# Three edits to a hybrid layer kernel: other step sizes in the down projections, wider column sums, two weight splits earlier

## The chip, the cores and the metric

One core of one Trainium2 chip runs the whole kernel in one launch. The metric is the time of an execution on the device in microseconds (us); less is better.

## What is computed

A decoder layer for 1024 tokens of width 1024, batch 1, all in float32. Each of its two feed-forward halves, with 2816 hidden columns, is

```python
def swiglu(h, w_gate, w_up, w_down):
    return (jax.nn.silu(h @ w_gate) * (h @ w_up)) @ w_down

def rms_norm(x, gain):
    xf = x.astype(jnp.float32)
    y = xf * lax.rsqrt(jnp.mean(xf * xf, axis=-1, keepdims=True) + EPS)
    return (y * gain.astype(jnp.float32)).astype(x.dtype)
```

The first half (stage 0) is followed by a mixer (four gated DeltaNet heads and four causal pooling groups), then by the second half (stage 1) and a final RMS norm. Every part is modulated by a vector c (adaLN).

## The kernel before

**Products in float32.** An operand is split into a high half of type fp32r, written by a cast on ScalarE (ACT) or GpSimd (POOL), and the low rest, which VectorE (DVE) writes as a subtraction. TensorE (PE) then issues three matmuls for each product of tiles: high × high, high × low, and low weights × high. They are one instruction each of 128x512 columns; a weight tile has a "split" with both halves.

**Seven products.** Gate, up and down are done as a 2 × 2 block scheme with seven products instead of eight (SLOTS: p1, p2, p5, p6, p3, p7, q4, in the order in which PE does them). The blocks of weights are combined on DVE (tiles pm, from raw or cv, which hold loaded blocks). The products go to PSUM banks: p1, p6, p7 and q4 use one bank of `mm` in turn, p2 a bank of `po`, p5 another, and p3 accumulates in p5's bank. So p6 waits until p1's content was read, p7 for p6's read, q4 for p7's, and p3 for p5's (the `flag("read", ...)` lines in `seven`).

**Pairs.** The 2816 hidden columns are 22 tiles, 11 pairs of tiles. Gate and up make one pair after the other, pair 1 first (PAIR0) and then in the order of PAIRS; the seven combinations of each pair's activation, split in halves, are what down multiplies. For the two pairs that are made last (DIRECT) DVE and ACT write these splits straight into their places in SBUF (`direct_task`): p5's into tiles U (high) and zs (low), p6 and p7 into G tiles, the others into H tiles. The other pairs' splits go to DRAM (`part_task`) and come back by DMA (`feed_task`). The eleventh pair is treated apart.

**Down.** It goes in steps. Step t works on the output pair d = t mod 4 with up to four pairs of hidden tiles; `nk` is the number of pairs. In the plan of before the steps have 1, 2, 3, 4, then 4, 4, 4, 4, then 4, 4, 3, 2 and 1 pairs. PE's row of products runs on from step to step, with the q4 of a step behind the p1 of the next. `down_read` lets DVE read a bank, scale it and add it to a residual tile A, which must have been loaded (`rest_load`, from `xpark` in stage 0 and from `rest` in stage 1); the tile that it is loaded into comes from a pool that activations use before.

**Order.** A planner in the program (`Order`), with costs for each operation and a rank for each task, decides before anything runs in which order each engine gets its instructions; each engine then takes them in that order. SyncE (SP) issues nearly all DMAs, also in a fixed order.

**Column sums.** For a norm the squares are summed over the width, which lies over partitions: `column_sums` multiplies a tile of 128x128 by ones on PE. In the finish (`finish`) there are three such sums of partial tiles for each group of rows, in separate columns, added by a reduction on DVE, followed by DVE's scale, POOL's power and the output. In `norm_task` there is one.

**Splits of weights.** `splits_task` spawns the tasks that split the weights ahead of PE (`unit_split`); a smaller rank is served sooner. The list `units` is that of the pair made first; its last two are the two halves of the up weights for the second tile of pair 1.

Of the kernel before, what the change touches and what calls it, by code (L numbers as in the profile page):

```python
# [11 lines left out]
ALU = mybir.AluOpType  # L12
AX = mybir.AxisListType

P = 128
D = 1024
# [10 lines left out]
PAIR0 = 1  # L27
PAIRS = (3, 4, 5, 6, 7, 8, 9, 10, 0, 2)

# [113 lines left out]
def hybrid_layer_kernel(  # L143
# [165 lines left out]

    def column_sums(parts, ps):  # L310
        for n in range(parts[0].shape[1] // P):
            for e, t in enumerate(parts):
                PE.matmul(ps[:, n : n + 1], lhsT=t[:, n * P : (n + 1) * P], rhs=ones[:, 0:1], start=(e == 0), stop=(e == len(parts) - 1))

# [437 lines left out]
    for st in range(2):  # L752
# [6 lines left out]
        for t in range(2 * NS):  # L759
            d = t % 4  # L760
            hi = min(NS, t + 1, at[d] + 4)
            if at[d] < hi:
                todo.append({"kind": "d", "d": d, "lo": at[d], "nk": hi - at[d], "w": wd})
                at[d] = hi
# [481 lines left out]
    def finish(st):  # L1246
# [3 lines left out]
        groups = ((0, 1), (1, 0))[i % 2]  # L1250
        kept = {}
        for g, b in enumerate(groups):
            banks = {}
# [9 lines left out]
            if g == 0:  # L1263
                yield flag("wrow")
                for m in range(n):
# [4 lines left out]
                    put(tags[m])  # L1270
        yield need("rec")
        sums = bank("rec")
        for j, e in enumerate((KT - 3, KT - 2, KT - 1)):
            yield flag("square", i, e)
            yield ("PE", 0.22 * n)
            column_sums((st["parts"][j - 1] if j else st["acc"],), sums[:, j * n : (j + 1) * n])
            put("cv" if j else "U")
        yield ("V", 0.3)
        r = small.tile([P, 4], F32, tag="rx", bufs=2, name=nm("rx"))[:, :n]
        V.tensor_reduce(r, sums[:, 0 : 3 * n].rearrange("p (j m) -> p m j", m=n), axis=AX.X, op=ALU.add)  # L1280
        V.tensor_scalar(r, r, 1.0 / D, EPS, op0=ALU.mult, op1=ALU.add)
        put("rec")
# [93 lines left out]
    def splits_task(units):  # L1376
        yield flag("w0", 1, 1, 1)
        yield from seven_splits(0)
        for key in [("last", dp) for dp in range(4)] + list(range(len(units))):
            yield need("split")  # L1380
            spawn(unit_split(key), 3)
        yield from seven_splits(1)
# [30 lines left out]
    def norm_task(h, i, parts, src, rank):  # L1413
# [5 lines left out]
        ps = bank("aux")  # L1419
        column_sums(parts[:1], ps)  # L1420
        yield ("V", 0.07)
        r = small.tile([P, 4], F32, tag="rx", bufs=2, name=nm("rx"))
        V.tensor_scalar(r, ps[:, 0:4], 1.0 / D, EPS, op0=ALU.mult, op1=ALU.add)
        put("aux")
# [658 lines left out]
```

## Time and profile before

| | |
|---|---|
| median of 3 runs | 1847.37 us (1847.31 to 1850.77) |
| the profiled execution | 1846.01 us |
| its span, first to last instruction | 1844.3 us |
| busy: PE, DVE, ACT, POOL | 97%, 76%, 41%, 15% of the span |
| mean granted clock of PE | 0.995 of full speed |

The profile is of one execution, so sums that are made from it stand against 1846.01. A name in it is that of the tiles without buffer numbers: `po<-H,split` is a matmul into a bank po with moving tile H and weight tile split. Nearly all operations are recorded by one helper and so have the same line (L161); stretches of time and names of tiles tell them apart. In timelines, equal neighbours are one row with a count.

### The profile page before, as it was taken

To read this page: it belongs to the slowest core of one execution; us is meant where nothing else is said; L and a number is where in the kernel's file an instruction comes from. 1 tells how busy PE (TensorE), PEld (TensorE's weight loads), DVE (VectorE), ACT (ScalarE), POOL (GpSimd) and SP (SyncE) were. 2 spreads that over 40 slices of the span, in tenths; PEclk is the share of its full clock that TensorE was granted. 3 is DMA by queue.
4 is the path that set the end of the run, shared out by engine and by line. 5 is a ranking of instruction groups with operands and counts; after the bars stand their busy time and mean duration, and the time that the engine had idled before them with its cause. 6 is when DMAs were issued, how large, how long until landed. Compare 5 with 4: busy or idle time off the path is not lost.

```text
span 1844.3 us, 25086 instructions
## 1 busy us (share of the span) xinstructions
PE 1793.7 (97%) x8527; PEld 1481.1 (80%) x8527; DVE 1398.6 (76%) x2434; ACT 759.9 (41%) x1504; POOL 283.5 (15%) x224
## 2 busy tenths in 40 slices
PE   7999999999899999999999999999999999999998
PEld 6788878888788877788888878878878888778877
DVE  5997888887778878988787666677787666786666
ACT  5454444454322224662443254354445444422223
POOL 2221121201100003120211122212111111100003
PEclk9999999999999999999999999999999999999999
DMA  9534665674679832331111155334455543667722
GB/s 323 176 126 162 221 220 191 189 236 127 201 248 329 302 102 98 103 79 43 31 48 49 41 172 157 99 120 145 153 186 180 181 141 116 207 206 254 237 77 98
DMA packets 307807, 293.81 MB, mean 159 GB/s; under 512 B 28061, under 2 KB 215506, under 8 KB 307680
## 3 DMA queue, kind: packets, MB, share of 16 engines
q1 hardware_dynamic: 307136, 291.09, 49.8%
q8 instruction: 67, 1.10, 0.2%
q0 software_dynamic: 544, 1.13, 0.2%
q14 instruction: 60, 0.49, 0.1%
HBM read 209.05 MB, written 83.10 MB: 158 GB/s over the span
## 4 chain that ended last, share of the span: by engine, by line
PE 84%; DVE 11%; issue 2%; ACT 1%; POOL 1%; DMA 1%; DVEq 0%; POOLq 0%; ACTq 0%
PE mm L161 47%; PE po L161 27%; PE aux L161 7%; PE rec L161 3%; DVE pm L161 2%; DVE split L161 2%; DVE A L161 2%; DVE ad L161 2%; DVE G L161 1%; DVE cv L161 1%; DVE H L161 1%; ACT A L161 0%; DMA G<-in_gdn_norm 0%; DVE zs L161 0%; ACT junk L161 0%
## 5 line engine op out<-in xcount | busy, mean ns | idle before, releaser
L161 PE MATMUL mm<-H,split 128*128 128x512 f32 (+1 forms) x3096 | 762.7, 394 | 10.5 <-DVE H L161 4.0
L161 PEld LDWEIGHTS mm<-H,split 128*128 128x128 f32 x3096 | 568.1, 189 | 127.7 <-issue 5.8
L161 PE MATMUL po<-H,split 128*128 128x512 f32 x1584 | 388.2, 392 | 4.5 <-DVE H L161 3.0
L161 PEld LDWEIGHTS po<-H,split 128*128 128x128 f32 x1584 | 297.1, 188 | 69.5 <-DVE H L161 4.2
L161 PE MATMUL mm<-G,split 128*128 128x512 f32 x1440 | 343.0, 390 | 4.3 <-ACT split L161 4.3
L161 PEld LDWEIGHTS mm<-G,split 128*128 128x128 f32 x1440 | 270.0, 188 | 61.2 <-ACT split L161 5.2
L161 ACT CAST split<-pm 128x512 fp32r<-128x512 f32 (+3 forms) x264 | 151.7, 582 | 329.0 <-DVE pm L161 321.7
L161 POOL TENSOR_TENSOR A<-A,A 128x512 f32<-128x512 f32 x80 | 131.9, 1659 | 690.8 <-DVE A L161 584.7
L161 DVE TENSOR_TENSOR split<-pm,split 128x512 fp32r<-128x512 f32 (+3 forms) x264 | 176.6, 676 | 45.1 <-ACT split L161 44.5
L161 ACT CAST split<-raw 128x512 fp32r<-128x512 f32 (+2 forms) x199 | 117.6, 595 | 193.0 <-PE mm L161 105.4
L161 PE MATMUL po<-U,split 128*128 128x512 f32 x480 | 155.5, 390 | 2.1 <-DVE A L161 2.0
L161 DVE SCALAR_TENSOR_TENSOR A<-mm,fg,A 128x512 f32<-128x512 f32 (+1 forms) x144 | 103.2, 719 | 63.6 <-PE mm L161 62.3
L161 DVE TENSOR_TENSOR split<-raw,split 128x512 fp32r<-128x512 f32 (+2 forms) x199 | 132.3, 675 | 21.4 <-ACT split L161 21.0
L161 DVE TENSOR_TENSOR A<-A,A 128x512 fp32r<-128x512 f32 (+1 forms) x180 | 124.1, 697 | 4.4 <-ACT A L161 1.2
L161 PEld LDWEIGHTS po<-U,split 128*128 128x128 f32 x480 | 90.1, 188 | 21.9 <-issue 1.7
L161 ACT CAST split<-cv 128x512 fp32r<-128x512 f32 (+1 forms) x96 | 57.1, 595 | 94.3 <-PE po L161 50.4
L161 DVE TENSOR_TENSOR A<-A,po 128x512 f32<-128x512 f32 x86 | 58.8, 684 | 46.4 <-PE po L161 43.7
L161 PE MATMUL po<-zs,split 128*128 128x512 f32 x240 | 93.4, 389 | 0.0
L161 DVE SCALAR_TENSOR_TENSOR ad<-ad,cs,ad 128x512 f32<-128x512 f32 x98 | 82.7, 844 | 3.2 <-DMA ad<-in_w_ada 2.4
L161 DVE TENSOR_TENSOR split<-cv,split 128x512 fp32r<-128x512 f32 (+1 forms) x96 | 62.7, 653 | 27.6 <-ACT split L161 27.6
L161 ACT CAST A<-A 128x512 fp32r<-128x512 f32 x120 | 72.8, 620 | 25.5 <-DVE A L161 25.2
L161 DVE SCALAR_TENSOR_TENSOR A<-po,fg,A 128x512 f32<-128x512 f32 x78 | 58.1, 749 | 32.2 <-PE po L161 31.5
(270 smaller groups left out, 1857.2 us busy)
## 6 DMA issues: line engine op xcount, KB each, us to landing
gd<-A SPq DMA_DIRECT2D x240, 256.0 KB, 3.9
H<-gd SPq DMA_DIRECT2D x144, 256.0 KB, 4.0
ad<-in_w_ada SPq DMA_DIRECT2D x112, 256.0 KB, 3.2
raw<-in_ffn_gate SPq DMA_DIRECT2D x88, 256.0 KB, 4.0
cv<-in_ffn_up SPq DMA_DIRECT2D x80, 256.0 KB, 4.3
G<-gd SPq DMA_DIRECT2D x64, 256.0 KB, 3.7
raw<-in_w_in SPq DMA_DIRECT2D x40, 256.0 KB, 3.1
cv<-in_ffn_down SPq DMA_DIRECT2D x32, 256.0 KB, 4.0
```

The source lines that it names most:

```text
L161: ins = f(*args, **kwargs)
```

## The change

There are three edits. The steps of down get 2, 3 and 3 pairs instead of 1, 2 and 3 at their start: 2, 3, 3, 4, then 3, 3, 4, 4, then 4, 4, 3, 2 and 1. With it pairs 2 and 3 change places in the order of making, so pair 3 is the last made, needed first as the fourth of a step with four pairs, and pair 2 the first made of PAIRS. The column sums use all 128 columns of ones, so each sum stands 128 times, in a block of PSUM of its own; in the finish three partial tiles accumulate in one block, which is set to zero beforehand, and no reduction is left. The last two units of the first pair get rank 1 instead of 3 in `splits_task`.

```diff
--- before.py
+++ after.py
@@ -25,7 +25,7 @@
 NS = NPAIR - 1
 
 PAIR0 = 1
-PAIRS = (3, 4, 5, 6, 7, 8, 9, 10, 0, 2)
+PAIRS = (2, 4, 5, 6, 7, 8, 9, 10, 0, 3)
 
 DIRECT = PAIRS[-2:]
 
@@ -307,10 +307,10 @@
             return gtile(8 + 2 * (k - KT // 2) + h)
         return ztile() if h else ad()
 
-    def column_sums(parts, ps):
-        for n in range(parts[0].shape[1] // P):
-            for e, t in enumerate(parts):
-                PE.matmul(ps[:, n : n + 1], lhsT=t[:, n * P : (n + 1) * P], rhs=ones[:, 0:1], start=(e == 0), stop=(e == len(parts) - 1))
+    def column_sums(t, ps, **flags):
+
+        for n in range(t.shape[1] // P):
+            PE.matmul(blk(ps, n), lhsT=blk(t, n), rhs=ones, skip_group_check=True, **flags)
 
     def row_diag(r):
         diag = cvt()
@@ -758,7 +758,7 @@
         at = [0] * 4
         for t in range(2 * NS):
             d = t % 4
-            hi = min(NS, t + 1, at[d] + 4)
+            hi = min(NS, t + (2, 2, 1)[min(t, 2)], at[d] + 4)
             if at[d] < hi:
                 todo.append({"kind": "d", "d": d, "lo": at[d], "nk": hi - at[d], "w": wd})
                 at[d] = hi
@@ -1249,6 +1249,11 @@
         tags = ("po", "po", "aux", "aux")[lo // P : lo // P + n]
         groups = ((0, 1), (1, 0))[i % 2]
         kept = {}
+        yield flag("row", i, 0)
+        yield need("rec")
+        sums = bank("rec")
+        yield ("V", 0.1 + 0.13 * n)
+        V.memset(sums[:, 0 : n * P], 0.0)
         for g, b in enumerate(groups):
             banks = {}
             for e in range(4 * g, 4 * g + 4):
@@ -1268,17 +1273,14 @@
                     kept[m] = ztile()
                     V.tensor_tensor(kept[m], banks[m], wrow[b], op=ALU.mult)
                     put(tags[m])
-        yield need("rec")
-        sums = bank("rec")
         for j, e in enumerate((KT - 3, KT - 2, KT - 1)):
             yield flag("square", i, e)
             yield ("PE", 0.22 * n)
-            column_sums((st["parts"][j - 1] if j else st["acc"],), sums[:, j * n : (j + 1) * n])
+            column_sums(st["parts"][j - 1] if j else st["acc"], sums, start=False, stop=j == 2)
             put("cv" if j else "U")
-        yield ("V", 0.3)
+        yield ("V", 0.2)
         r = small.tile([P, 4], F32, tag="rx", bufs=2, name=nm("rx"))[:, :n]
-        V.tensor_reduce(r, sums[:, 0 : 3 * n].rearrange("p (j m) -> p m j", m=n), axis=AX.X, op=ALU.add)
-        V.tensor_scalar(r, r, 1.0 / D, EPS, op0=ALU.mult, op1=ALU.add)
+        V.tensor_scalar(r, sums[:, 0 : n * P : P], 1.0 / D, EPS, op0=ALU.mult, op1=ALU.add)
         put("rec")
         yield ("G", 1.0)
         G.tensor_tensor(r, r, neghalf[:, :n], op=ALU.pow)
@@ -1378,7 +1380,7 @@
         yield from seven_splits(0)
         for key in [("last", dp) for dp in range(4)] + list(range(len(units))):
             yield need("split")
-            spawn(unit_split(key), 3)
+            spawn(unit_split(key), 1 if key in (len(units) - 2, len(units) - 1) else 3)
         yield from seven_splits(1)
         for dp in range(4):
             yield need("split")
@@ -1417,10 +1419,10 @@
         yield need("cv")
         yield ("PE", 0.9)
         ps = bank("aux")
-        column_sums(parts[:1], ps)
+        column_sums(parts[0], ps, start=True, stop=True)
         yield ("V", 0.07)
         r = small.tile([P, 4], F32, tag="rx", bufs=2, name=nm("rx"))
-        V.tensor_scalar(r, ps[:, 0:4], 1.0 / D, EPS, op0=ALU.mult, op1=ALU.add)
+        V.tensor_scalar(r, ps[:, 0:HT:P], 1.0 / D, EPS, op0=ALU.mult, op1=ALU.add)
         put("aux")
         put("U")
         yield ("G", 1.0)
```

What this does to the engines' orders is shown at three places. The first is DVE at the start of the first down projection, before, in stage 0 (A tiles are residuals, `mm_914` and the banks `po` are the first step's products, `pm` is a sum of weight blocks, `H0_1` is q4's split of pair 0):

```order
L161 SCALAR_TENSOR_TENSOR A12_850_4213<-mm_914_4511,fg0_164,A12_850_4213 128x512 [waits DMAHW2_49,PE_49]
L161 SCALAR_TENSOR_TENSOR A12_850_4213<-po_917_4520,fg0_164,A12_850_4213 128x512 [waits DVE_49,PE_49]
L161 SCALAR_TENSOR_TENSOR A10_853_4216<-po_920_4530,fg0_164,A10_853_4216 128x512 [waits PE_49]
L161 SCALAR_TENSOR_TENSOR A4_851_4214<-mm_914_4511,fg0_164,A4_851_4214 128x512 [waits PE_49]
L161 TENSOR_TENSOR H0_1_915_4513<-A1_857_4225,H0_1_915_4513 128x512 [waits Activation_49]
L161 SCALAR_TENSOR_TENSOR A4_851_4214<-po_920_4530,fg0_164,A4_851_4214 128x512 [waits DVE_49,PE_49]
L161 TENSOR_TENSOR pm_926_4558<-raw_866_4277,raw_873_4311 128x128
L161 TENSOR_TENSOR split_918_4523<-cv_891_4380,split_918_4523 128x256 [waits DMAHW0_49,Activation_49]
L161 TENSOR_TENSOR split_921_4533<-raw_875_4317,split_921_4533 128x128 [waits Activation_49]
L161 TENSOR_TENSOR split_929_4564<-pm_926_4558,split_929_4564 128x128 [waits Activation_49]
```

and with the change:

```order
L161 TENSOR_TENSOR H0_1_915_4513<-A1_857_4225,H0_1_915_4513 128x512 [waits Activation_49]
L161 SCALAR_TENSOR_TENSOR A12_850_4213<-mm_914_4511,fg0_164,A12_850_4213 128x512 [waits DMAHW2_49,PE_49]
L161 TENSOR_TENSOR pm_921_4539<-raw_866_4277,raw_873_4311 128x256
L161 TENSOR_TENSOR split_919_4530<-cv_891_4382,split_919_4530 128x384 [waits DMAHW0_49,Activation_49]
L161 SCALAR_TENSOR_TENSOR A12_850_4213<-po_918_4527,fg0_164,A12_850_4213 128x512 [waits DVE_49,PE_49]
L161 TENSOR_TENSOR split_925_4552<-pm_921_4539,split_925_4552 128x256 [waits Activation_49]
L161 SCALAR_TENSOR_TENSOR A10_853_4216<-po_922_4541,fg0_164,A10_853_4216 128x512 [waits PE_49]
L161 TENSOR_TENSOR split_924_4548<-raw_875_4318,split_924_4548 128x256
L161 SCALAR_TENSOR_TENSOR A4_851_4214<-mm_914_4511,fg0_164,A4_851_4214 128x512 [waits PE_49]
```

The sum pm of raw_866 and raw_873, for p7, stood behind five reads and H0_1, and now stands behind one read. The second place is DVE in the third step of the same projection, before (`A9<-mm` is the read of p6, `A13<-po_985` that of p5, `zs` the low half of p5's split of the pair made last):

```order
L161 TENSOR_TENSOR zs_944_4611<-A13_919_4528,U_943_4610 128x512 [waits Pool_49]
L161 SCALAR_TENSOR_TENSOR A0_937_4587<-mm_969_4699,fg0_164,A0_937_4587 128x512 [waits PE_49]
L161 SCALAR_TENSOR_TENSOR A7_906_4475<-mm_934_4581,fg0_164,A7_906_4475 128x512 [waits DMAHW7_49,PE_49]
L161 TENSOR_TENSOR pm_982_4754<-raw_912_4498,raw_931_4569 128x384
L161 TENSOR_TENSOR split_981_4747<-cv_957_4651,split_981_4747 128x512 [waits DMAHW5_49,Activation_49]
L161 SCALAR_TENSOR_TENSOR A0_937_4587<-po_980_4743,fg0_164,A0_937_4587 128x512 [waits DVE_49,PE_49]
L161 TENSOR_TENSOR split_983_4760<-pm_982_4754,split_983_4760 128x384 [waits Activation_49]
L161 TENSOR_TENSOR split_986_4769<-raw_933_4579,split_986_4769 128x384 [waits Activation_49]
L161 TENSOR_TENSOR G5_949_4626<-A5_924_4546,G4_948_4625 128x512 [waits Pool_49]
L161 SCALAR_TENSOR_TENSOR A13_979_4742<-po_985_4764,fg0_164,A13_979_4742 128x512 [waits DMAHW4_49,PE_49]
L161 TENSOR_TENSOR split_988_4784<-cv_968_4697,split_988_4784 128x512 [waits DMAHW0_49,Activation_49]
L161 SCALAR_TENSOR_TENSOR A9_977_4726<-mm_969_4699,fg0_164,A9_977_4726 128x512 [waits DMAHW2_49,PE_49]
```

and with the change:

```order
L161 SCALAR_TENSOR_TENSOR A0_935_4600<-po_980_4785,fg0_164,A0_935_4600 128x512 [waits PE_49]
L161 TENSOR_TENSOR split_986_4809<-raw_929_4571,split_986_4809 128x384 [waits Activation_49]
L161 TENSOR_TENSOR zs_945_4629<-A13_917_4525,U_944_4628 128x512 [waits Pool_49]
L161 TENSOR_TENSOR G7_948_4638<-A5_923_4544,G6_947_4637 128x512 [waits Pool_49]
L161 TENSOR_TENSOR H7_1_953_4654<-A11_880_4331,H7_1_953_4654 128x512
L161 TENSOR_TENSOR split_988_4825<-cv_968_4716,split_988_4825 128x512 [waits DMAHW0_49,Activation_49]
L161 SCALAR_TENSOR_TENSOR A9_969_4726<-mm_973_4750,fg0_164,A9_969_4726 128x512 [waits DMAHW1_49,PE_49]
L161 TENSOR_TENSOR pm_992_4844<-cv_963_4686,cv_965_4701 128x512 [waits DMAHW7_49,DMAHW6_49]
L161 TENSOR_TENSOR G15_956_4667<-A8_890_4377,G14_955_4666 128x512 [waits Pool_49]
L161 SCALAR_TENSOR_TENSOR A13_989_4830<-po_985_4806,fg0_164,A13_989_4830 128x512 [waits DMAHW7_49,DVE_49]
L161 TENSOR_TENSOR split_993_4847<-pm_992_4844,split_993_4847 128x512 [waits Activation_49]
```

The read of p5 stood ahead of that of p6; it now stands three places behind, and the split into zs stands after the read of p2 (`A0<-po_980`). The third is DVE in stage 1 at the last up tile of pair 1, before (raw_2293 and raw_2294 are its two weight units, G and zs combinations of activations):

```order
L161 TENSOR_TENSOR zs_2335_11096<-ad_2232_10584,U_2334_11095 128x512 [waits Activation_49,Pool_49]
L161 TENSOR_TENSOR split_2336_11102<-raw_2302_10914,split_2336_11102 128x512 [waits DMAHW5_49,Activation_49]
L161 TENSOR_TENSOR G1_2339_11111<-G9_2315_10995,G0_2338_11110 128x512 [waits Activation_49]
```

followed, after twelve others, by

```order
L161 SCALAR_TENSOR_TENSOR G12_2253_10666<-G12_2253_10666,mod6_158,G13_2323_11027 128x512
L161 TENSOR_TENSOR split_2342_11124<-raw_2293_10872,split_2342_11124 128x512 [waits DMAHW2_49]
L161 SCALAR_TENSOR_TENSOR G14_2260_10696<-G14_2260_10696,mod6_158,G15_2325_11034 128x512
L161 TENSOR_TENSOR split_2345_11136<-raw_2294_10879,split_2345_11136 128x512 [waits DMAHW3_49]
```

and with the change:

```order
L161 TENSOR_TENSOR zs_2335_11096<-ad_2232_10584,U_2334_11095 128x512 [waits Activation_49,Pool_49]
L161 TENSOR_TENSOR split_2336_11102<-raw_2293_10872,split_2336_11102 128x512 [waits DMAHW2_49,Activation_49]
L161 TENSOR_TENSOR split_2338_11110<-raw_2294_10879,split_2338_11110 128x512 [waits DMAHW3_49,Activation_49]
L161 TENSOR_TENSOR split_2339_11116<-raw_2302_10914,split_2339_11116 128x512 [waits DMAHW5_49,Activation_49]
L161 TENSOR_TENSOR zs_2341_11123<-ad_2234_10592,U_2340_11122 128x512 [waits Activation_49,Pool_49]
```

The splits of raw_2293 and raw_2294 now come right behind a split into zs.

## Rows read from the trace of the kernel before

**Rows 1.** The page: busy time, share of span, instructions of TensorE.

```profile
PE 1793.7 (97%) x8527; PEld 1481.1 (80%) x8527; DVE 1398.6 (76%) x2434; ACT 759.9 (41%) x1504; POOL 283.5 (15%) x224
```

**Rows 2.** Timeline of PE, 470 to 530: start, length, operation, count, [idle before, releaser].

```profile
482.16 0.84 PE L161 MATMUL po<-H,split 128*128 128x512 f32 x3
...
484.79 0.93 PE L161 MATMUL po<-H,split 128*128 128x512 f32 x3 [0.42 <-DVE A L161]
487.89 0.97 PE L161 MATMUL mm<-G,split 128*128 128x512 f32 x3 [2.17 <-ACT split L161]
...
501.44 2.11 PE L161 MATMUL mm<-H,split 128*128 128x512 f32 x8 [2.02 <-DVE H L161]
...
511.71 0.74 PE L161 MATMUL po<-H,split 128*128 128x512 f32 x2 [0.46 <-DVE H L161]
...
514.38 4.92 PE L161 MATMUL mm<-H,split 128*128 128x512 f32 x21
519.14 2.88 PE L161 MATMUL po<-H,split 128*128 128x512 f32 x12
```

**Rows 3.** Timelines of DVE and of POOL, 484 to 489.

```profile
486.48 0.97 DVE L161 TENSOR_TENSOR pm<-raw,raw 128x128 f32<-128x128 f32 x1
...
486.04 1.26 POOL L161 TENSOR_TENSOR A<-A,A 128x512 f32<-128x512 f32 x1 [5.10 <-DVE H L161]
```

**Rows 4.** Timeline of PE, the same start in stage 1.

```profile
1600.04 0.84 PE L161 MATMUL po<-H,split 128*128 128x512 f32 x3
...
1605.76 1.38 PE L161 MATMUL mm<-G,split 128*128 128x512 f32 x3 [2.17 <-ACT split L161]
1606.93 3.44 PE L161 MATMUL mm<-H,split 128*128 128x512 f32 x9
...
1638.49 1.75 PE L161 MATMUL po<-H,split 128*128 128x512 f32 x7
```

**Rows 5.** Windows: busy us of PE, PEld, DVE, ACT, POOL (instructions), granted clock, DMA.

```profile
1606.00:1608.00 2.00, 2.00 (x6) 1.55 (x6) 1.97 (x6) 1.16 (x4) 0.00 (x0) 0.53 0.67 199
...
1204.00:1206.00 2.00, 2.00 (x5) 1.61 (x6) 1.08 (x2) 0.00 (x0) 0.00 (x0) 0.50 0.40 114
```

**Rows 6.** Timeline of DVE, 497 to 512: the pitch of operations back to back.

```profile
507.22 0.69 DVE L161 TENSOR_TENSOR G<-A,G 128x512 fp32r<-128x512 f32 x1
507.83 0.74 DVE L161 SCALAR_TENSOR_TENSOR A<-po,fg,A 128x512 f32<-128x512 f32 x1
508.49 0.68 DVE L161 TENSOR_TENSOR split<-cv,split 128x512 fp32r<-128x512 f32 x1
```

**Rows 7.** DMA issues of 498 to 522: count, KB each, median us to landing.

```profile
A<-xpark SPq DMA_DIRECT2D x7, 256.0 KB, 2.9
```

**Rows 8.** Timeline of PE, 1190 to 1225, stage 1.

```profile
1199.94 0.61 PE L161 MATMUL mm<-H,split 128*128 128x512 f32 x2
1203.87 17.52 PE L161 MATMUL mm<-H,split 128*128 128x512 f32 x70 [3.31 <-DVE split L161]
1221.23 4.01 PE L161 MATMUL po<-H,split 128*128 128x512 f32 x17
```

**Rows 9.** Timeline of DVE there.

```profile
1203.14 0.68 DVE L161 TENSOR_TENSOR split<-raw,split 128x512 fp32r<-128x512 f32 x1
```

**Rows 10.** Timeline of PE, two stretches: 54 to 60, and the finish.

```profile
56.53 1.05 PE L161 MATMUL rec<-ones,pm 128*128 128x128 f32 x8
57.34 0.48 PE L161 MATMUL mm<-H,split 128*128 128x512 f32 x1
...
1815.73 0.95 PE L161 MATMUL rec<-ones,U 128*128 128x1 f32 x8
1816.54 1.93 PE L161 MATMUL rec<-ones,cv 128*128 128x1 f32 x16
```

**Rows 11.** Timeline of DVE, the end of the finish.

```profile
1836.99 0.16 DVE L161 TENSOR_REDUCE rx<-rec 128x2 f32<-128x6 f32 x1 [1.76 <-PE rec L161]
```

**Rows 12.** Timeline of SP's DMA issues, 440 to 515.

```profile
480.33 2.14 SPq L1165 DMA_DIRECT2D H<-gd  x4
```

## The prediction

> **What bounds the kernel now.** I read the page's busy time first. TensorE (PE) is busy 97% of the span [rows 1], so time can be won only where PE stands still or runs at its lower clock. I then read PE's timeline and looked for brackets, each of which is an idle time with the engine that ended it. Three stretches that the change touches stand out.
>
> The first is the start of the down projection of stage 0, where the steps have 1, 2 and 3 pairs [rows 2]. The reader is to see a wait of 2.17 us for a weight split, one of 2.02 us for an H split on VectorE (DVE), and two small ones of 0.42 and 0.46. At full pace 21 matmuls take 514.38 to 519.14, 4.76 us, 0.2267 each. From 482.16 (the second product of the first step) to 519.14 (the second of the fourth) there are 18 + 42 + 63 + 12 = 135 matmuls, worth 30.6 us. They take 36.98, so **6.4 us are lost**.
>
> The reason for the first wait is on DVE: the weight sum for p7 stands behind the reads of p1, p2, p5, p6 and p3, starts only at 486.48, and takes 0.97 us, while GpSimd (POOL) works on an operation of 1.26 us [rows 3]. A one-pair step gives PE 21 matmuls, 4.76 us. DVE has seven bank reads in it at a pitch of 0.66 [rows 6] and some eleven short splits and sums, which I put at 0.2 to 0.25 each (an estimate: the operation four times as wide has a pitch of 0.61 there): 7 us. DVE cannot keep up with one pair.
>
> The second is the same start in stage 1 [rows 4]: 1600.04 to 1638.49 is 38.45 us for the same 135 matmuls, **7.85 us lost**. The wait of 2.17 us is there again, but the nine matmuls behind it take 3.44 us, and the granted clock of 1606 to 1608 is 0.53 [rows 5], near the lower of the two levels (1.2 of 2.4 GHz). That is the 1.5 us by which stage 1 is worse.
>
> The third is the last up tile of the first pair in stage 1 [rows 8]. Two of the three matmuls of a product's first part are issued at 1199.94. The third needs the low half of the weight and waits 3.31 us for DVE, which writes it from 1203.14 on [rows 9]. To 1221.23 there are 72 matmuls, worth 16.3 us; they take 21.29, so **5.0 us are lost**: 3.5 standing still, and 1.5 in the lower clock, 0.50 in 1204 to 1206 [rows 5].
>
> **The change part by part.** *Step sizes and the last-made pair.* Both plans have 13 steps with 40 pair parts, so the same number of matmuls. Let S be the start of the first step's p1, some 481.5 in stage 0 and 1599.4 in stage 1. With two pairs a product is 6 × 0.2267 = 1.36 us, so p1, p2, p5, p6 and p3 end at S+1.36, 2.72, 4.08, 5.44 and 6.80, and p7 begins there. In the new order of DVE the sum for p7 stands right behind p1's read (the first place shown of the orders): the read ends at S+2.2, and the sum, a split, p2's read and the low half of p7's weights are done at about S+4.6. They are there 2 us early, so the 2.17 goes, and with it the 0.42. The tight place is p3 of that step, which accumulates in p5's bank: p5's read ends at S+5.3, against S+5.44.
>
> The last-made pair is needed only in the fourth step, from S+36 on. DVE writes its H tiles at S+17 to 19 and its zs at S+30, so the 2.02 and the 0.46 go. Everything that the swapped pairs issue moves with them: pair 2 is now written to DRAM and fed back, as pair 3 was, at the same places of SP's queue up to the third step. It is needed by the third pair of the second step, from S+9 on; the last of these feeds, the tiles of q4, are issued at 480.33 to 482.47 [rows 12], so by S+1. By this the whole 6.4 and 7.85 us are freed.
>
> *What takes their place.* The zs split of the last-made pair now stands behind p2's read of the third step (the second place shown). It reads the tile into which the residual A13 is loaded next, so that load, and the p5 read that adds to A13, stand later as well: the p5 read is now behind p6's read and two sums. PE's p3 needs the p5 read, and DVE takes its instructions in order. p6 ends at S+31.96; then 0.2 to DVE, the p6 read 0.66, two sums 0.60 each [rows 6], the p5 read 0.74 and 0.15 back to PE: S+34.9. Where PE went from p6 straight to p3 before, it **waits 2.9 us in each stage**. By the load: zs done at S+29.9, issue at S+30.2, landing 2.9 us later by the median [rows 7], S+33.1, which is 0.9 before DVE gets there; a load 1.8 us slower than the median makes the wait 3.8. I take 2.9, since DVE's order alone gives it.
>
> Does this wait lower the clock? The 2.17 did so in stage 1 and not in stage 0, the 2.02 in neither (by its eight matmuls in 2.11 us), the 3.31 did. By these rows I take a drop of 1.5 us, the price in stage 1, in one of the two stages; none and both are kept for the range. The Trainium skill, page "TensorE: Matmul & The Clock Gate", section "Why this matters for your kernels", says that idle gaps between bursts of matmuls bring the half clock. By that alone both stages would drop, and the forecast would be 1.5 us later; the trace agrees for the 3.31.
>
> Down: −6.4 + 2.9 = −3.5 in stage 0, −7.85 + 2.9 + 1.5 = −3.45 in stage 1.
>
> *Splits first.* Only DVE was late. In its new order (the third place shown) the two low halves stand 14 and 15 places earlier, at 0.6 each over 8 us, so the third matmul finds its weights: −5.0. What stands behind them, the combinations of activations, is late by two operations, 1.2 us. They are first needed by p6, which is 48 + 24 + 24 + 24 = 120 matmuls, 27 us, after 1199.94, so this reaches nothing; if it did, it would cost those 1.2. Two gate loads that wait for the raw tiles of these splits go out sooner on SP, ahead of three loads of the AdaLN weights, for which nothing waits in the stretch.
>
> *Column sums.* Eight 128x1 matmuls take 0.81 us from their start to the next group's (1815.73 to 1816.54); eight 128x128 ones of the front take 0.81 as well (56.53 to 57.34) [rows 10]. By their durations it is 0.95 against 1.05. The change makes 80 such matmuls wider, 32 in the norms ahead of the mixer and of stage 1 and 48 in the finish, so the price is between 0 and 10 × 0.10 = 1.0 us. The memsets, three, each at most the 0.69 of a 128x512 operation [rows 6], lie in DVE's waits ahead of the sums, 1.76 us before the last one; without that cover they would cost 2.1 together. The reduction of 0.16 us on the path to the end [rows 11] goes. I take 0 for the part, from −0.2 to +1.0. The Trainium skill, the same page, section "Back-to-back issue gap", gives about 60 cycles for 1 to 64 columns and 134 for 128. By that the 80 would cost 80 × 74 cycles, 2.5 us (an estimate from that page), and the forecast would be 1837.9; the equal pitches in the trace disagree.
>
> Sum: −3.5 − 3.45 − 5.0 + 0 = −12.0 us. On the profiled execution's own 1846.01 us (1844.3 of span and 1.7 around it) that gives 1834.0. The median of the runs, 1847.37, is 1.36 above that execution, so I predict **1835.4** for the median.
>
> **The rivals.** *No new wait.* If p3 of the third step does not stand still, only the gains stay: −6.4 − 7.85 − 5.0 = −19.2, 1828.2. For it: three-pair steps give PE 14.3 us and leave DVE time to spare. Against: p6's read cannot begin before p6 ends, and the p5 read is behind it. Chance 0.15.
>
> *A dearer wait.* The A13 load lands 1.8 us late (3.8 of wait), both stages drop to the lower clock, and the sums cost their 1.0: −6.4 + 5.3 − 7.85 + 5.3 − 5.0 + 1.0 = −7.65, 1839.7. For it: two waits of the trace did cost clock. Against: the median load is early by 0.9. Chance 0.17.
>
> *No difference.* The same inversion of p5's and p6's reads on DVE holds PE for 2.9 us in two more steps of each stage: −12.0 + 4 × 2.9 = −0.4, 1847.0. For it: DVE's order is a new one until the down projection's middle. Against: I find that inversion in one step only. Chance 0.07.
>
> *Slower.* One mechanism: the A13 load decides p3 of the third step. Beyond S+34 each us of its landing is a us of wait in each stage. The rest is worth −19.2, so the kernel is slower by 3.7 once the two waits together pass 22.9, 11.4 each, which is a landing twelve us after the issue. At 13 us it is −19.2 + 2 × 12.1 = +5.0, 1852.4. For it: the load is issued only when the zs split is done, just in time. Against: the median is 2.9. Chance 0.04.
>
> **How the numbers follow.** Forecast 0.57, no new wait 0.15, dearer 0.17, no difference 0.07, slower 0.04. The forecast's own range is 1832 to 1838: a clock drop in none or both, 1.5 either way, and the sums' −0.2 to +1.0. The range that I give reaches to the second and third case: 1827.5 to 1840.5. A measurement of this kernel can tell about 0.2%, 3.7 us, from no change. Faster by more than that: 0.57 + 0.15 + 0.17, less 0.01 for what lies between the cases, 0.88; within it 0.07 + 0.01 = 0.08; slower 0.04.
>
> **What would show it.** In the profile after: no bracket of 2.17 or 2.02 us in the first steps of either down projection, and one new bracket of about 2.9 us in the third step, before p3 on `po`, ended by DVE A, with the read of `mm` and two sums ahead of the read of `po` on DVE; a clock near 0.5 behind it in one stage. No bracket at 1200, and 72 matmuls in 16.3 us. Eight column sums in 0.81 us. The prediction is wrong if PE goes from that p6 straight to p3, if the new bracket is ended by a DMA, or if the sums run at another pitch.

## The result and the profile after

The changed kernel takes 1838.5 us in the median of 5 runs (1835.2 to 1841.67), the kernel before 1847.37 (1847.25 to 1850.77) beside it. The ratio is 0.9948 with a 95% interval of 0.9931 to 0.9964, that is 9.6 us less, between 6.6 and 12.7. The forecast was 1835.4 with a range of 1827.5 to 1840.5, and 0.88 for a gain over 0.2%. The profiled execution took 1837.93 us, 8.1 below that of before; where these 8.1 come from is read in the rows that follow. The ratios leave out two executions, of 5794.9 and 7100.37 us, one each in the second and the fourth experiment.

The page after: busy time by engine.

```profile
PE 1791.9 (98%) x8527; PEld 1481.6 (81%) x8527; DVE 1398.9 (76%) x2434; ACT 759.8 (41%) x1504; POOL 282.1 (15%) x224
```

PE idles 44.3 us of the span instead of 50.6 (1836.2 − 1791.9, against [rows 1]).

PE's timeline at the start of stage 0's down projection answers to [rows 2].

```profile
482.71 1.52 PE L161 MATMUL po<-H,split 128*128 128x512 f32 x6
...
486.84 1.60 PE L161 MATMUL po<-H,split 128*128 128x512 f32 x6
488.28 1.52 PE L161 MATMUL mm<-G,split 128*128 128x512 f32 x6
...
511.40 2.20 PE L161 MATMUL mm<-G,split 128*128 128x512 f32 x9
516.40 3.67 PE L161 MATMUL po<-H,split 128*128 128x512 f32 x9 [2.80 <-DVE A L161]
519.87 2.49 PE L161 MATMUL mm<-G,split 128*128 128x512 f32 x9
...
526.97 2.88 PE L161 MATMUL po<-H,split 128*128 128x512 f32 x12
```

The waits of 2.17, 2.02, 0.42 and 0.46 are gone: p3 and p7 of the first step, at 486.84 and 488.28, have no bracket. One is new: nine matmuls of p6 begin at 511.40, and p3, the `po<-H` row at 516.40, waits 2.80 us for DVE's A. The reader is to see the row's length too: nine matmuls take 3.67 us here, against 2.20 in the row ahead and 2.49 in the row behind. From 482.71 (p2 of the first step) to 526.97 (p2 of the fourth) there are now 174 matmuls, 39.45 us at 0.2267 each. They take 44.26, so 4.8 us are lost where it was 6.4.

The same start in stage 1, which answers to [rows 4]:

```profile
1595.65 1.52 PE L161 MATMUL po<-H,split 128*128 128x512 f32 x6
...
1629.37 3.87 PE L161 MATMUL po<-H,split 128*128 128x512 f32 x9 [2.80 <-DVE A L161]
...
1639.91 0.39 PE L161 MATMUL po<-H,split 128*128 128x512 f32 x1
```

The same 44.26 us for the same 174 matmuls: 4.8 lost, where it was 7.85. The granted clock (the number ahead of the last two) in windows behind the two waits, beside [rows 5]:

```profile
518.00:520.00 2.00, 2.00 (x6) 1.52 (x6) 0.00 (x0) 0.00 (x0) 0.00 (x0) 0.50 0.49 131
...
1631.00:1633.00 2.00, 2.00 (x6) 1.55 (x5) 0.00 (x0) 0.00 (x0) 0.00 (x0) 0.50 0.39 131
```

So the clock fell to the lower level, 0.50, in both stages. DVE's timeline in the third step of stage 0 shows why PE waited:

```profile
509.56 0.75 DVE L161 SCALAR_TENSOR_TENSOR A<-po,fg,A 128x512 f32<-128x512 f32 x1 [0.22 <-PE po L161]
...
510.69 0.69 DVE L161 TENSOR_TENSOR zs<-A,U 128x512 fp32r<-128x512 f32 x1
...
513.64 0.75 DVE L161 SCALAR_TENSOR_TENSOR A<-mm,fg,A 128x512 f32<-128x512 f32 x1 [0.46 <-PE mm L161]
514.31 0.68 DVE L161 TENSOR_TENSOR pm<-cv,cv 128x512 f32<-128x512 f32 x1
514.91 0.69 DVE L161 TENSOR_TENSOR G<-A,G 128x512 fp32r<-128x512 f32 x1
515.51 0.75 DVE L161 SCALAR_TENSOR_TENSOR A<-po,fg,A 128x512 f32<-128x512 f32 x1
```

The read of p2 (`A<-po` at 509.56) is followed by the split into zs and others, and DVE then waits 0.46 us for p6. The read of p6 at 513.64, two operations, and only then p5's read, at 515.51. PE's p3 follows at 516.40. The bank of p5 had been ready since p6 began, at 511.40. No row of DVE has a bracket that names a DMA. The load that p5's read needs is the first of these on SP's queue:

```profile
511.41 6.39 SPq L1176 DMA_DIRECT2D A<-xpark  x5
```

It is issued at 511.41, as soon as the split into zs has ended (510.69 and 0.69), and lands 2.8 us later, at 514.2, so 1.3 us before the read begins. The order on DVE therefore ends the wait. The load is next behind it: a read put ahead of p6's could not have begun before 514.2 either, and with the 0.9 us from the read's start to PE's (515.51 to 516.40) p3 would still have waited some 1.5 us (an estimate from these rows).

The last up tile of the first pair in stage 1, beside [rows 8]:

```profile
1199.81 16.48 PE L161 MATMUL mm<-H,split 128*128 128x512 f32 x72
1216.13 5.60 PE L161 MATMUL po<-H,split 128*128 128x512 f32 x24
```

All 72 matmuls run on, in 16.32 us instead of 21.29. The wait is gone with nothing in its place.

Two places show a new or a longer wait. The first is the norm ahead of the mixer. Before, on PE and then on POOL, the diagonal `aux<-cv` began at 705.57 after a wait of 1.21 us:

```profile
700.53 0.95 PE L161 MATMUL aux<-ones,acc 128*128 128x1 f32 x8
...
705.57 1.10 PE L161 MATMUL aux<-cv,ones 128*128 128x512 f32 x2 [1.21 <-DVE cv L161]
...
711.17 2.00 PE L161 MATMUL po<-H,split 128*128 128x512 f32 x5 [2.09 <-DVE H L161]
```

```profile
701.34 1.29 POOL L161 TENSOR_TENSOR acc<-acc,cv 128x512 f32<-128x512 f32 x1 [1.17 <-ACT cv L161]
702.59 1.03 POOL L161 TENSOR_TENSOR rx<-rx,neghalf 128x4 f32<-128x4 f32 x1
```

With the change:

```profile
699.46 1.05 PE L161 MATMUL aux<-ones,acc 128*128 128x128 f32 x8
...
705.85 1.10 PE L161 MATMUL aux<-cv,ones 128*128 128x512 f32 x2 [2.60 <-DVE cv L161]
...
711.17 2.21 PE L161 MATMUL po<-H,split 128*128 128x512 f32 x5 [1.90 <-DVE H L161]
```

```profile
700.27 2.65 POOL L161 TENSOR_TENSOR acc<-acc,cv 128x512 f32<-128x512 f32 x2 [1.17 <-ACT cv L161]
702.88 1.03 POOL L161 TENSOR_TENSOR rx<-rx,neghalf 128x4 f32<-128x4 f32 x1
```

The eight matmuls of the sums began at 699.46, about 1.1 us sooner than before (700.53, the 128x1 group), but the diagonal comes at 705.85, after a wait of 2.60. POOL's power `rx` starts only at 702.88, behind two accumulations of squares that begin at 700.27, where it was one that began at 701.34. The next wait of PE ends at 711.17 in both executions. The 1.1 us by which the changed kernel was ahead at the sums are used up there. The second place is the finish:

```profile
1807.61 1.06 PE L161 MATMUL rec<-ones,U 128*128 128x128 f32 x8
1808.50 1.95 PE L161 MATMUL rec<-ones,cv 128*128 128x128 f32 x16
...
1825.86 0.97 PE L161 MATMUL mm<-H,split 128*128 128x256 f32 x6 [0.58 <-DVE A L161]
```

The sums over 128 columns keep a pace of about 0.1 us per matmul: eight take 0.89 us here (1807.61 to 1808.50) and 0.81 in the norm, against 0.81 in [rows 10]. There is a wait of 0.58 us that the kernel before did not have. In time nothing is lost: from the first of these sums to the end of the span it is 28.6 us in both executions (1807.61 to 1836.2, and 1815.73 to 1844.3).

By landmarks of the two traces the difference for the same work is this: −0.6 at the end of stage 0's down projection, −0.1 behind the mixer's norm, −5.1 behind the last tile, −8.1 at the end of stage 1's first steps, and −8.1 at the end.

### The profile page after: what moved, and what is told of

Same layout as the page of the kernel before. It is cut to its first block, busy times and chain, and to the rows that moved or that the text cites. A ratio compares the mean times of both kernels' runs of the same rounds, so it can differ in the third digit from the quotient of the medians.

```text
span 1836.2 us, 25080 instructions
## 1 busy us (share of the span) xinstructions
PE 1791.9 (98%) x8527; PEld 1481.6 (81%) x8527; DVE 1398.9 (76%) x2434; ACT 759.8 (41%) x1504; POOL 282.1 (15%) x224
## 4 chain that ended last, share of the span: by engine, by line
PE 85%; DVE 10%; issue 2%; ACT 1%; POOL 1%; DMA 1%; DVEq 0%; POOLq 0%; SPq 0%; ACTq 0%
PE mm L161 48%; PE po L161 27%; PE aux L161 7%; PE rec L161 3%; DVE pm L161 2%; DVE ad L161 2%; DVE A L161 1%; DVE split L161 1%; DVE G L161 1%; DVE cv L161 1%; DVE zs L161 0%; DVE H L161 0%; ACT A L161 0%; DMA G<-in_conv_w 0%; ACT junk L161 0%
## 5 line engine op out<-in xcount | busy, mean ns | idle before, releaser
L161 ACT CAST split<-raw 128x512 fp32r<-128x512 f32 (+3 forms) x199 | 117.6, 595 | 189.2 <-PE mm L161 106.4
L161 DVE TENSOR_TENSOR split<-raw,split 128x512 fp32r<-128x512 f32 (+3 forms) x199 | 131.6, 672 | 20.3 <-ACT split L161 19.9
L161 ACT CAST split<-cv 128x512 fp32r<-128x512 f32 (+2 forms) x96 | 57.1, 595 | 91.5 <-PE po L161 55.8
L161 DVE TENSOR_TENSOR split<-cv,split 128x512 fp32r<-128x512 f32 (+2 forms) x96 | 62.7, 653 | 28.3 <-ACT split L161 28.3
```

What stands on the lines that cost most here:

```text
L161: ins = f(*args, **kwargs)
```

## The experiments

All times are medians, and each ratio is against the kernel before on the same chip. The theory, A below, is that each edit does what the rows show, that the new wait is the order of p5's and p6's reads on DVE, and that the wide sums cost through POOL's order. The rivals are in the expectations.

**Only the earlier splits** (of the three edits, against the kernel before).

```diff
-            spawn(unit_split(key), 3)
+            spawn(unit_split(key), 1 if key in (len(units) - 2, len(units) - 1) else 3)
```

> Of the three edits only the earlier splits of the first pair's last tile. Theory A (each part of the sum stands where it was seen): the wait of 3.31 us and the slow matmuls behind it go and nothing takes their place, 5.0 us below the kernel before, 1842.4. Rival (gain given back behind it, by the activation combinations that come 1.2 us later): 3.8 us or less below. In the profile: 72 matmuls from about 1200 in 16.3 us by A.

Measured: 1841.09 us, ratio 0.9966 (0.9955 to 0.9978), 6.3 us less, between 4.1 and 8.3. PE's timeline there:

```profile
1201.44 16.48 PE L161 MATMUL mm<-H,split 128*128 128x512 f32 x72
```

72 matmuls in a row, which win the 5.0 us at that place: this execution is 1.5 us behind the one of [rows 8] at their start and 3.5 ahead at the next tile's (1217.76 against 1221.23). It is the slowest of the six, and it loses most of that lead again in stage 1's down projection, where waits that this edit leaves alone are followed by more slow matmuls. One of them:

```profile
1618.58 3.67 PE L161 MATMUL mm<-H,split 128*128 128x512 f32 x8 [2.01 <-DVE H L161]
```

The same eight take 2.11 us in the kernel before. The gain in time is that of the median. Its interval holds the 5.0 and leaves out the rival's 3.8 or less. That it lies above 5.0 would fit the price of the old wait, which varies: the 70 matmuls behind it took 17.52 us in [rows 8], and 17.6 to 19.0 in the six experiments that still have it. Theory A stands.

**Only the step sizes with the swapped pairs.**

```diff
-PAIRS = (3, 4, 5, 6, 7, 8, 9, 10, 0, 2)
+PAIRS = (2, 4, 5, 6, 7, 8, 9, 10, 0, 3)
...
-            hi = min(NS, t + 1, at[d] + 4)
+            hi = min(NS, t + (2, 2, 1)[min(t, 2)], at[d] + 4)
```

> Of the three edits only the step sizes with the swapped pairs; column sums and splits as before. Theory A: stage 1 wins 3.0 us as in the changed kernel, and stage 0, without the wider sums, keeps the 0.6 us that it is ahead at the end of the down projection, so 3.6 us below before, 1843.8; the power of the mixer's norm stands one place earlier on GpSimd and the wait for its diagonal is about 1.3 us. Rival B (the norm of the mixer swallows whatever stage 0 wins, sums or not): 3.0 below, and the power no earlier than in the changed kernel. The wait of 2.8 us before p3 of the third step stays in both stages by either.

Measured: 1843.32 us, ratio 0.9972 (0.9960 to 0.9983), 5.2 us less, between 3.1 and 7.4. The third step of stage 0 and the mixer's norm on PE:

```profile
516.75 3.24 PE L161 MATMUL po<-H,split 128*128 128x512 f32 x9 [2.80 <-DVE A L161]
```

```profile
704.82 1.10 PE L161 MATMUL aux<-cv,ones 128*128 128x512 f32 x2 [1.21 <-DVE cv L161]
...
710.41 1.43 PE L161 MATMUL po<-H,split 128*128 128x512 f32 x5 [2.09 <-DVE H L161]
```

The wait of 2.80 is there, with nine slow matmuls behind it. The diagonal waits 1.21 us, as before, and not 2.60: the power is not late without the wide sums. It comes 0.75 us sooner than in the kernel before (705.57), so what stage 0 won goes through the norm, and rival B, that the norm swallows it by itself, falls. The time alone does not separate 3.6 from 3.0.

**Only the wide column sums**: `column_sums` and its callers as in the changed kernel, everything else as before.

```diff
-                PE.matmul(ps[:, n : n + 1], lhsT=t[:, n * P : (n + 1) * P], rhs=ones[:, 0:1], start=(e == 0), stop=(e == len(parts) - 1))
+            PE.matmul(blk(ps, n), lhsT=blk(t, n), rhs=ones, skip_group_check=True, **flags)
```

> Of the three edits only the wider column sums. Theory A: eight matmuls keep their 0.81 us, but GpSimd's power in the first half of the mixer's norm falls behind one more accumulation of squares, as in the changed kernel, so the diagonal comes 0.9 to 1.3 us later and the kernel is 0.5 to 1.3 us slower than before, 1848.3. Rival B (the sums are free, and the power's place costs nothing): within 0.3 us of before.

Measured: 1848.17 us, ratio 1.0000 (0.9992 to 1.0009), between 1.5 less and 1.7 more. The mixer's norm:

```profile
702.46 1.05 PE L161 MATMUL aux<-ones,acc 128*128 128x128 f32 x8
...
708.84 1.10 PE L161 MATMUL aux<-cv,ones 128*128 128x512 f32 x2 [2.60 <-DVE cv L161]
```

The wait of 2.60 us for the diagonal comes with the wide sums alone. POOL's order shows the cause, one row of difference (- before, + wide sums):

```
 L161 TENSOR_TENSOR acc_6448<-acc_6448,cv_6489 128x512
+L161 TENSOR_TENSOR acc_6448<-acc_6448,cv_6494 128x512
 L161 TENSOR_TENSOR rx_6497<-rx_6497,neghalf 128x4
-L161 TENSOR_TENSOR acc_6448<-acc_6448,cv_6494 128x512
```

The time is by itself undecided: the interval holds the 1.0 us of theory A and zero. From the first sum to the second diagonal the trace has 23.9 us here (702.46 to 726.35) and 22.9 before (700.53 to 723.41), which is the sign of theory A. The whole of it lies in the waits: from the first sum to the end of the next wait it is 11.7 us here (to 714.17) and 10.6 before (to 711.17), and from there to the next sums 6.5 in both. The changed kernel has the same 11.7 (699.46 to 711.17).

**The residuals in the order of need.** The changed kernel, with p5's residual loaded second instead of fourth.

```diff
-                for d in (2 * p, 2 * p + 1):
-                    for h in range(2):
-                        spawn(rest_load(st, d, h), 2.5)
+                for d, h in ((2 * p, 0), (2 * p + 1, 1), (2 * p, 1), (2 * p + 1, 0)):
+                    spawn(rest_load(st, d, h), 2.5)
```

> The changed kernel, with the residual tiles of down loaded in the order in which the reads need them (p1's, p5's, p6's, q4's instead of p1's, p6's, q4's, p5's), which in DVE's order puts p5's read of the third step ahead of p6's. Theory A (the new wait of 2.8 us is p5's read standing behind p6's): the wait and the slow matmuls behind it go in both stages, 4.5 us each, and the kernel comes to 1838.5 - 9 = 1829.5; if the mixer's norm swallows part of stage 0's, 1834. Rival C (the new wait is the residual's load landing late): a wait of 2 us or more stays before p3, now ended by DVE behind the load, and the time stays within 2 us of 1838.5.

Measured: 1830.24 us, ratio 0.9904 (0.9890 to 0.9918), 8.3 us below the changed kernel's median. PE in the third step of stage 0, and DVE there:

```profile
512.34 2.20 PE L161 MATMUL mm<-G,split 128*128 128x512 f32 x9
514.38 2.20 PE L161 MATMUL po<-H,split 128*128 128x512 f32 x9
516.42 2.20 PE L161 MATMUL mm<-G,split 128*128 128x512 f32 x9
```

```profile
511.63 0.68 DVE L161 TENSOR_TENSOR zs<-A,U 128x512 fp32r<-128x512 f32 x1
512.54 0.75 DVE L161 SCALAR_TENSOR_TENSOR A<-po,fg,A 128x512 f32<-128x512 f32 x1 [0.23 <-PE po L161]
...
514.64 0.75 DVE L161 SCALAR_TENSOR_TENSOR A<-mm,fg,A 128x512 f32<-128x512 f32 x1
```

PE goes from p6 (512.34) straight to p3 (514.38), and all three groups of nine take 2.20. On DVE the first `A<-po` behind the split into zs is p5's read, at 512.54, ahead of p6's at 514.64. The zs split still ends late, at 512.3, and p5's read begins 0.2 us behind it, so its load no longer waits for that split. Rival C, a wait that stays and is ended by the load, falls. But the edit moves the load as well as the read, so it does not tell the two apart: that the order ended the wait of 2.80 is shown by the changed kernel's own rows, and that the order alone would have been enough is not shown. The gain of 8.3 us is near the 9.6 that the first steps of the two stages had lost together.

**The step sizes without the swap**: in the kernel before, the `hi` line alone.

> The kernel before with the new step sizes alone: pairs are made in the old order, so pair 2 is the last made and is needed as the third pair of the second step. In DVE's order its H split then stands four operations behind the read of p3 of the first step, about S+9.7 against a need at S+9.5, and p5's read of the third step stands ahead of p6's. Theory A (the swap of the pairs, not the step sizes, brings the wait of 2.8 us; the steps of two pairs alone remove those of 2.17 and 2.02): no wait over 1 us in the first four steps of either projection, some 12 us below before, 1836. Rival D (the swap is needed: the direct splits of the last-made pair come late for the second step): waits of 2 us or more there by DVE H or G, no gain beyond 5 us, 1843 or more.

Measured: 1839.84 us, ratio 0.9954 (0.9942 to 0.9967), 8.5 us less, between 6.1 and 10.7. PE's waits in stage 0 (stage 1 has the same, 1.27 and 0.80):

```profile
494.40 2.11 PE L161 MATMUL mm<-H,split 128*128 128x512 f32 x8 [1.26 <-DVE H L161]
...
511.14 0.73 PE L161 MATMUL mm<-H,split 128*128 128x512 f32 x2 [0.80 <-DVE H L161]
```

No wait of 2.8 us; two smaller ones for the direct H splits of pair 2. They stand where rival D put them, but are shorter than its 2 us. By the medians the new step sizes alone win more than with the swap (8.5 against 5.2), though the two intervals overlap. Theory A's mechanism holds; its 12 us was too much, because these two waits, 2.06 us in each stage, come in place of the old ones of 2.02 and 0.46.

**The swap without the step sizes**: the `PAIRS` line alone.

> The kernel before with pairs 2 and 3 swapped alone, steps of 1, 2, 3 and 4. Theory A: the wait of 2.17 us (weights of p7 in the one-pair step) stays, those of 2.02 and 0.46 go, and a wait of 2.8 to 3 us before p3 of the third step comes, since p5's read stands behind p6's here too: by the waits +0.4 us a stage, with the clock between -1 and +3 in all, so 1847 to 1851. Rival (the swap alone wins the 2.02 and 0.46 and costs nothing): 5 below, 1843.

Measured: 1858.89 us, ratio 1.0055 (1.0041 to 1.0069), 10.2 us more. Both forecasts missed. PE in the third step, and DVE before it:

```profile
515.70 4.15 PE L161 MATMUL po<-H,split 128*128 128x512 f32 x9 [6.27 <-DVE A L161]
```

```profile
508.73 0.69 DVE L161 TENSOR_TENSOR H<-A,H 128x512 fp32r<-128x512 f32 x1
...
510.54 0.69 DVE L161 TENSOR_TENSOR zs<-A,U 128x512 fp32r<-128x512 f32 x1
...
512.95 0.74 DVE L161 SCALAR_TENSOR_TENSOR A<-mm,fg,A 128x512 f32<-128x512 f32 x1
...
514.81 0.74 DVE L161 SCALAR_TENSOR_TENSOR A<-po,fg,A 128x512 f32<-128x512 f32 x1
```

The wait before p3 is 6.27 us in both stages, not 3. The planner serves the last-made pair's splits when they are needed, and that is now later: the first H split at 508.73, zs at 510.54. The tiles come free late, the residuals are loaded late (from 509.48 on), and p6's read (`A<-mm`, 512.95) and p5's (514.81) stand behind these splits and behind each other. The same, with the load order of the fourth experiment:

> The swap alone (steps of 1, 2, 3, 4) with the residuals loaded in the order of need. In DVE's order p5's read of the third step then stands two places sooner, ahead of p6's, but still behind the late H, zs and G splits of pair 3. Theory A (the swap alone waits 6.27 us because DVE splits pair 3 late, so the residual's tile is free late, and the inversion adds to it): the wait falls to about 4.4 us in each stage, two operations and a read less, 1855. Rival (all of the 6.27 is the inversion): no wait, 1845.

Measured: 1854.69 us, ratio 1.0039 (1.0025 to 1.0052).

```profile
512.17 4.18 PE L161 MATMUL po<-H,split 128*128 128x512 f32 x9 [4.41 <-DVE A L161]
```

The wait is 4.41 us, as expected: the load order takes 1.9 of the 6.27 away, and the 4.4 that stay are read as the late splits.

**The load order alone**, in the kernel before.

> The kernel before with the residuals in the order of need and nothing else. Theory A (the load order pays only where the changed plan puts p5's read behind p6's, and before it is ahead already): within 0.1% of before. Rival (the load order is worth some us by itself): 3 or more below.

Measured: 1847.73 us, ratio 0.9999 (0.9990 to 1.0008). By itself it does nothing. It wins 8.3 us where steps and pairs are both changed, and takes 1.9 us off a wait where the pairs alone are (the experiment before this one).

**Powers and sums.** The program holds PE, DVE and ACT to the planner's order (`pinned`), but not POOL, whose instructions may be put into another order when the program is built. Here is the kernel with the load order, and the square sums and powers of the norms kept on POOL in the planner's order too:

```diff
-            G.tensor_tensor(parts[0], parts[0], sq, op=ALU.add)
+            tc.keep_in_program_order(G.tensor_tensor(parts[0], parts[0], sq, op=ALU.add))
...
-        G.tensor_tensor(r, r, neghalf[:, 0:4], op=ALU.pow)
+        tc.keep_in_program_order(G.tensor_tensor(r, r, neghalf[:, 0:4], op=ALU.pow))
```

> The kernel with the residuals loaded in the order of need, and the powers and square sums of the norms kept on GpSimd in the order of the program, which puts the power of the mixer's norm ahead of two accumulations again. Theory A (the wider sums cost through the power's place): the wait for the diagonal falls from 2.60 to 1.2 us or less and the time by 1.0 to 1.4, 1829. Rival B (nothing hangs on it): 1830.2.

Measured: 1827.39 us, ratio 0.9886 (0.9873 to 0.9900); the wait for the diagonal is 0.54 us instead of 2.60. Next, the load order with the narrow sums of before:

> Step sizes, swap, earlier splits and residuals in the order of need, but the column sums of before (one column each and a reduction). Theory A: the wait for the diagonal in the mixer's norm is 1.2 us instead of 2.60, and the new 0.58 us in the finish goes; the reduction of 0.2 us comes back: 1.0 to 1.5 below the one with wide sums, 1829. Rival B (sums are free): 1830.2.

Measured: 1828.80 us, ratio 0.9895 (0.9881 to 0.9908). Then both, the narrow sums and the kept order:

> New step sizes, swap, earlier splits, residuals in the order of need, column sums of before, powers kept in program order on GpSimd. Theory A: the wait for the diagonal of the mixer's norm falls from 1.21 to about 0.5 us as with wide sums, and the finish keeps its short waits: 0.5 to 1 below the same without the kept order (1828.8), 1828. Rival: the diagonal isn't what PE waits for in the end, 1828.8.

Measured: 1827.88 us, ratio 0.9890 (0.9877 to 0.9904). The mixer's norm on PE, first of the kernel with narrow sums, then with narrow sums and kept order:

```profile
702.53 1.10 PE L161 MATMUL aux<-cv,ones 128*128 128x512 f32 x2 [1.21 <-DVE cv L161]
...
708.12 1.41 PE L161 MATMUL po<-H,split 128*128 128x512 f32 x5 [2.08 <-DVE H L161]
```

```profile
699.20 1.10 PE L161 MATMUL aux<-cv,ones 128*128 128x512 f32 x2 [0.39 <-DVE cv L161]
...
704.08 1.42 PE L161 MATMUL po<-H,split 128*128 128x512 f32 x5 [1.38 <-DVE H L161]
```

The diagonal's wait falls from 1.21 to 0.39 us and the next one from 2.08 to 1.38. The lowest median is 1827.39, with wide sums, some 20 us below the kernel before and 11 below the changed one. The three medians lie within 1.4 us, and their intervals overlap with each other and with that of 1830.24. That the power's place costs 1.5 to 2 us of waits is shown by the traces; that it costs the same in time is likely, not shown.

**No swap**, with everything else of the kernel with narrow sums and the load order.

> New step sizes, earlier splits, residuals in the order of need, column sums of before, but the pairs made in the old order. Theory A (the swap is worth the waits of 1.26 and 0.80 us that the new steps alone keep, in both stages): 4 to 6 us more than the same with the swap (1828.8), so 1834. Rival (these waits are hidden by something else that comes later): 1829.

Measured: 1834.07 us, ratio 0.9926 (0.9912 to 0.9939), 5.3 us above the same with the swap. Without the swap the waits of 1.26 and 0.80 are there in both stages, 4.1 us together and most of the 5.3. With the old load order the swap cost 3 by the medians (5.2 against 8.5 won).

## Why the prediction came out as it did

*The old waits.* Right: all four go, in both stages. The step sizes remove those of 2.17 and 0.42 (the fifth experiment; with the swap alone, the sixth, both stay), and the swap is needed for the other two, which the step sizes alone turn into 1.26 and 0.80. The 6.4 and 7.85 us were in fact freed.

*The new wait.* Right in place, cause and size: 2.80 us before p3 of the third step against 2.9, p3 at S+35.0 (S is 482.71 − 1.36) against S+34.9. DVE's order ended it, as said, and the load was where the prediction had it: it landed at S+32.9 against S+33.1. What the prediction did not say is that the order made only the last 1.3 us of the 2.80; without the inversion the load would have kept some 1.5 (the estimate above).

*The clock behind it.* This term was mis-sized. I took one drop in the two stages; both dropped. The nine matmuls cost 1.5 and 1.7 us more than at full clock, and some 0.3 more follow in the next row of stage 0. Stage 0's first steps therefore won 1.6 us and not 3.5; stage 1's won 3.0 and not 3.45. The rival of a dearer wait had this step right, by its clock and not by its load. The Trainium skill, page "TensorE: Matmul & The Clock Gate", section "Why this matters for your kernels", as the prediction reads it, would have had both stages drop, and here the trace agrees. That section speaks of gaps above a length, a condition that the prediction left out; the traces show a drop behind the 2.80 us in all four places looked at, and behind waits of 2.0 to 2.2 us in some.

*What follows stage 0.* This step failed. I counted what the first steps of stage 0 win as won to the end. In the trace 0.6 of the 1.6 us is left at the end of that projection. The trace names one cause, two waits of 0.2 us for `ad` at 595 and 612 that the kernel before does not have; the rest stays open. At the norm's sums it is 1.1 us again, and the late power on POOL takes 1.0 of it.

*The column sums.* The price on PE was right, next to nothing. The part was set to nothing without a look at POOL's order, and there the wide sums move one power behind one more accumulation: alone they cost the same stretch the same 1.1 us (the third experiment), and with the order on POOL kept the wait goes (0.54). In time this is not separable. The 2.5 us estimated from the Trainium skill, page "TensorE: Matmul & The Clock Gate", section "Back-to-back issue gap", lie outside the interval of that run, which ends at 1.7 more. The section gives its figures for a matmul by itself, and says that in a stream the weight loads count too, which the prediction left out.

*The last tile.* Right: 5.0 in the trace, as predicted, and 6.3 (4.1 to 8.3) by itself in the time.

Of the forecast −12.0, the profiled pair shows −8.1: 3.4 of the 3.5 in stage 0 are missing, and 0.45 in stage 1. In stage 0 the clock took 1.9, the rest of the projection 1.0 and the norm 1.0, and 0.5 came back between these two. The median is inside the range given, 0.5 outside the forecast's own. That range's lower end, 1832, does not follow from the terms named for it, which give 1833.7. And the two low halves of the last tile stand 15 and 16 places earlier in the orders shown, not 14 and 15; nothing hangs on it.

## What to carry to other kernels

A wait that is removed by giving a step more work comes back where the next in-order engine meets two reads in the wrong order; look there for the operand that is loaded last though it is needed second, since loading four tiles in the order of need was worth 8.3 us, nearly as much as the whole change (9.6). Two edits of one plan can have opposite signs by themselves: here the swap alone cost 10 us, and with new steps and loads it won 5. A gain in an early stage counts only if the next serial chain, here sum, power, diagonal, starts earlier as well.

## What was not expected of the hardware

The same wait does not always cost the same clock. In the mixer's norm a wait of 2.09 us stands ahead of the same matmuls in three executions. From its end to the next sums PE takes 6.53 us in the kernel before (five matmuls in 2.00), 6.50 in the first experiment (the five in 1.41, but six behind them in 2.65) and 4.90 in the second (the five in 1.43, the six in 1.52). A wait of 2.01 or 2.02 in the kernel with the splits alone left eight at 2.11 in stage 0 and at 3.67 in stage 1. The 2.80 was followed by the lower level in all four places looked at (3.67 and 3.87 for nine in the changed kernel, 3.24 and 3.87 in the second experiment). Runs of the changed kernel range over 6.5 us, and the mean granted clock with them: 0.998 in that of 1835.2, 0.992 in that of 1841.67.
